# Last product of layer 2: four column blocks over all tokens, four over the left and the right tokens

## The chip, the cores and the metric

The kernel runs on one core of a Trainium2 chip. The metric is the device time of one execution in microseconds: the median of three runs for the kernel before, and one further execution that was profiled. The engines are TensorE (PE, and PEld for its weight loads), VectorE (DVE), ScalarE (ACT), GpSimd (POOL) and SyncE (SP); SP and ACT also issue the DMA transfers of this kernel.

## The reference

Two layers work on 512 tokens of width 1024, then a final RMSNorm. Cut to the part that matters here:

```
h = rmsnorm(x, norm_g)
proj = einsum('bsd,dc->bsc', h, w_in)          # feeds three mixers and three gates
...
pb = einsum('nbsc,ncd->nbsd', ys, w_branch)    # three branch products
gates = sigmoid(gl.reshape(B, S, 3, D))
merged = einsum('bsnd,nbsd->bsd', gates, pb)
x = x + einsum('bsd,de->bse', merged, w_out)   # the last product of a layer
...
out = rmsnorm(x, final_g)                      # after layer 2
```

## The kernel before

All activations lie transposed: features on the 128 partitions, the 512 tokens along the row. A product is done in three matmuls for float32 accuracy: each operand is split into a hi and a lo half, and `mm3` (lines 416 to 419) adds hi x hi, hi x lo and lo x hi into PSUM. The last product of a layer, `i_out` (line 789), makes eight column blocks `e` of 128 output features from eight input chunks `kc`, so 24 matmuls for a block. "Merged" chunks are the inputs: `mg` for chunks 0 to 5, `mgh` and `mgl` (hi and lo) for 6 and 7.

Weights arrive as units of 512 KB (`raw`, two buffers, loaded on SP's queue by `load`, line 138). Each unit has two halves, and `slot` (line 151) splits a half: ScalarE copies it rounded (`whi`, line 159), VectorE or, for one in five, GpSimd subtracts (`wlo`, line 160). There are six `whi` buffers and five `wlo` buffers (lines 154 and 155). `take` hands split halves to a product, `spent` says that one is used, and `ahead` then writes further splits into the program. A load buffer comes free when both halves of its unit are split.

In layer 1 a block covers all 512 tokens, and its halves are spent as it goes. In layer 2 the program goes through the eight blocks twice, first for the left 256 tokens (`LT`), then for the right 256 (`RT`), so that the final norm of the left tokens can be computed beside the right blocks. The weights therefore stay for both passes. Blocks 0 to 2 stay in the `whi` and `wlo` buffers; blocks 3 to 6 go into `xh` and `xl`, the layer's old input activations (no longer read by then), and block 7 into `mh` and `ml`:

```
if g[0] == "O" and g[1] >= NSLOT // 2 and l == DEPTH - 1:
    k = 2 * g[1] + i - NSLOT
    if k < KC:
        dst = xh[:, k, :], xl[:, k, :]
```

For each block the residual `xr` is loaded on ACT's queue (line 795, two buffers), VectorE evicts PSUM into `xf` and adds it (line 810, PSUM tiles `ps_to` in four banks), ScalarE squares it (line 275) and GpSimd adds the squares up (line 279). `final` (line 821) then sums the squares over the features by matmuls with a column of ones (line 394), takes the power on GpSimd (line 401), spreads the result over the partitions (lines 408 and 413), scales the eight blocks on VectorE (line 826) and writes them out, four on SP's queue and four on ACT's (line 827). `final(LT)` stands in the program behind the first right block.

Every engine runs its instructions in the order that a scheduler has set when the program is built. `slot` asks for high priority (`PRIO`), so splits come early in that order. A scheduled instruction waits at the head of its engine's queue until its inputs and buffers are ready, and what stands behind it waits too.

Of the kernel before, what the change touches and what calls it, by code (L numbers as in the profile page):

```python
# [14 lines left out]
ALU = mybir.AluOpType  # L15
# [5 lines left out]
S = 512  # L21
DEPTH = 2
KC = D // P
# [72 lines left out]
NSLOT = 6  # L96
# [3 lines left out]
def hybrid_kernel(ctx: ExitStack, tc, xT, posr, wpack, tabs, cvec, pvec, rvec, lamv, sguw, outT):  # L100
    nc = tc.nc
    V, A, G, T = nc.vector, nc.scalar, nc.gpsimd, nc.tensor
# [16 lines left out]
    def t2k(tag, bufs=2, dt=F32, name=None):  # L119
        return tmp.tile([P, S], dt, tag=tag, bufs=bufs, name=name or tag)  # L120

    def t4k(tag, bufs, dt=F32, name=None):
        return att.tile([P, 2, S], dt, tag=tag, bufs=bufs, name=name or tag)
# [7 lines left out]
    def ps_to():  # L131
        return to_p.tile([P, S], F32, tag="to", name="ps_to")
# [5 lines left out]
    def load():  # L138
        while loaded[0] < min(split_up[0] + RAWB, NU * DEPTH):
            raws[loaded[0]] = raw = wp.tile([P, 1024], F32, tag="raw", bufs=RAWB, name="raw")  # L140
            nc.sync.dma_start(out=raw, in_=wpack[loaded[0]])
            loaded[0] += 1
# [8 lines left out]
    def slot(src, dst=None):  # L151
        if dst is None:
            made[0] += 1
            hi = wp.tile([P, S], F32R, tag="whi", bufs=NSLOT, name="whi")
            lo = wp.tile([P, S], F32R, tag="wlo", bufs=NSLOT - 1, name="wlo")
        else:
            hi, lo = dst
        with tc.high_priority(offset=PRIO):
            A.activation(out=hi, in_=src, func=AF.Copy)  # L159
            (G if made[0] % LOMOD == 0 else V).tensor_tensor(out=lo, in0=src, in1=hi.bitcast(F32), op=ALU.subtract)  # L160
        slots.append((hi, lo))

    def weights():
        for l in range(DEPTH):
            for g in GROUPS:
                u = split_up[0]
                load()
                if g[0] == "S":
                    r1, r2 = raws.pop(u), raws.pop(u + 1)
                    a11, a12, a21, a22 = r1[:, :S], r1[:, S:], r2[:, :S], r2[:, S:]  # L170
                    t12, t34 = t4k("pr", 2, name="t12"), t4k("pr", 2, name="t34")
                    s1, s2, s3, s4 = t12[:, 0, :], t12[:, 1, :], t34[:, 0, :], t34[:, 1, :]
                    slot(a11)
                    yield
                    slot(a12)
                    yield
                    slot(a22)
                    with tc.high_priority(offset=PRIO):
                        SE[0].tensor_tensor(out=s1, in0=a21, in1=a22, op=ALU.add)
                        SE[1].tensor_tensor(out=s2, in0=s1, in1=a11, op=ALU.subtract)  # L180
                        SE[2].tensor_tensor(out=s3, in0=a11, in1=a21, op=ALU.subtract)
                        SE[3].tensor_tensor(out=s4, in0=a12, in1=s2, op=ALU.subtract)
                    split_up[0] += 2
                    load()
                    yield
                    for src in (s2, s3, s1, s4):
                        slot(src)
                        yield
                    continue
                raw = raws.pop(u)  # L190
                for i in range(2):
                    dst = None
                    if g[0] == "O" and g[1] >= NSLOT // 2 and l == DEPTH - 1:
                        k = 2 * g[1] + i - NSLOT
                        if k < KC:
                            dst = xh[:, k, :], xl[:, k, :]
                        else:
                            k = 2 * (k - KC)
                            dst = tuple(t[:, 0, k : k + 2, :].rearrange("p k c -> p (k c)") for t in (mh, ml))
                    slot(raw[:, i * S : i * S + S], dst)  # L200
                    if i == 1:
                        split_up[0] += 1
                        load()
                    yield

    wgen = weights()

    def ahead(n=NSLOT):
# [4 lines left out]
    def take(n):  # L213
        while len(slots) < n:
            next(wgen)
        out = slots[:n]
        del slots[:n]
        return out

    def spent(n):  # L220
        used[0] += n
        ahead()
# [14 lines left out]
    xh = per.tile([P, KC, S], F32R, name="xh")  # L237
    xl = per.tile([P, KC, S], F32R, name="xl")
    mh = per.tile([P, 4, 4, 256], F32R, name="mh")
    ml = per.tile([P, 4, 4, 256], F32R, name="ml")  # L240
# [163 lines left out]
    def rms_spread(rp):  # L404

        n = rp.shape[-1]
        dg = t2k("ob", name="dg")[:, : n * P]
        V.tensor_tensor(
            out=dg.rearrange("p (b j) -> p b j", b=n), in0=ident.unsqueeze(1).to_broadcast([P, n, P]),
            in1=rp.unsqueeze(2).to_broadcast([P, n, P]), op=ALU.mult,  # L410
        )
        bc = ps_s()[:, : n * P]
        T.matmul(bc, lhsT=ones, rhs=dg, start=True, stop=True)
        return bc

    def mm3(ps, wh, wl, mh, ml, first, last):
        T.matmul(ps, lhsT=wh, rhs=mh, start=first, stop=False)  # L417
        T.matmul(ps, lhsT=wh, rhs=ml, start=False, stop=False)  # L418
        T.matmul(ps, lhsT=wl, rhs=mh, start=False, stop=last)  # L419
# [5 lines left out]
    def proj_T(ps, src):  # L425
        for i, (wh, wl) in enumerate(take(2)):
            wh, wl = (w.rearrange("p (k c) -> p k c", k=4) for w in (wh, wl))
            for k in range(4):
                kc = 4 * i + k
                mm3(ps, wh[:, k, :], wl[:, k, :], *src(kc), kc == 0, kc == KC - 1)  # L430
                if k == 3:
                    spent(1)
                yield 0.65
# [61 lines left out]
    LT, RT = slice(0, 256), slice(256, 512)  # L495
# [62 lines left out]
    def layer(l, xu, parts):  # L558
        last = l == DEPTH - 1
# [226 lines left out]
        def merged(kc):  # L786
            return mg[kc // 2][0][:, kc % 2, :], mg[kc // 2][1][:, kc % 2, :]

        def i_out():
            xn[0] = x_ = X()  # L790
            parts = []
            for c in [LT, RT] if last else [slice(0, S)]:
                for e in range(8):
                    xr = t2k("sh", name="xr")[:, c]
                    nc.scalar.dma_start(out=xr, in_=(xT[e, :, c] if l == 0 else x1d[e, :, c]))
                    ps = ps_to()[:, c]
                    if not last:
                        yield from proj_T(ps, merged)
                    else:
                        if c is LT:  # L800
                            parts.append(take(2))
                        for i, (wh, wl) in enumerate(parts[e]):
                            wh, wl = (w.rearrange("p (k c) -> p k c", k=4) for w in (wh, wl))
                            for k in range(4):
                                kc = 4 * i + k
                                mh, ml = merged(kc)
                                mm3(ps, wh[:, k, :], wl[:, k, :], mh[:, c], ml[:, c], kc == 0, kc == KC - 1)
                                yield 0.325
                    xf = (x_.raw(e) if c.start == 0 else x_.f[e // 2][:, e % 2, :])[:, c]
                    V.scalar_tensor_tensor(out=xf, in0=ps, scalar=0.5, in1=xr, op0=ALU.mult, op1=ALU.add)  # L810
                    if last:
                        x_.square(e, c, True)
                    else:
                        x_.take(e, l + 1)
                        nc.sync.dma_start(out=x1d[e], in_=xf)
                    if c is RT and e == 0:
                        final(LT)
            if last:
                final(RT)

        def final(c):
            x_ = xn[0]
            bc = rms_spread(rms_sum([x_.ss[:, c], x_.sq[:, c]]))
            for e in range(KC):
                xf = x_.f[e // 2][:, e % 2, c]
                V.scalar_tensor_tensor(out=xf, in0=xf, scalar=fg[:, e : e + 1], in1=bc, op0=ALU.mult, op1=ALU.mult)
                (nc.sync, nc.scalar)[e % 2].dma_start(out=outT[e, :, c], in_=xf)
# [222 lines left out]
    x1d = dr.tile([KC, P, S], F32, name="x1d")  # L1050
# [88 lines left out]
```

## Time and profile before

| what | us |
|---|---|
| median of three runs (lowest 1148.14, highest 1153.46) | 1151.81 |
| profiled execution | 1150.43 |
| its span on the core | 1148.7 |
| TensorE busy in the span | 1107.1 (96%) |
| VectorE busy | 821.6 (72%) |
| ScalarE busy | 601.7 (52%) |
| GpSimd busy | 515.7 (45%) |

The span holds all instructions of the execution; 1.73 us of the execution lie outside it. The mean granted clock of TensorE over the span is 0.987 of full speed. A busy share is an average over stages, and the product of this change fills only the last part of the span, from about 1076 to 1138 us. A matmul's end in the trace is modelled and overlaps the next one, so the time of a matmul in a stream is read as the distance between two starts.

### The profile page before, as it was taken

Reading aid. Unit: us, or ns where it says so; the run is one execution under the profiler, and the core shown is the slowest. Engines: PE = TensorE matmul, PEld = TensorE weight load, DVE = VectorE, ACT = ScalarE, POOL = GpSimd, SP = SyncE. Lnnn points to the kernel's source line nnn. Section 1 sums busy time; section 2 is a strip of 40 time slices with the busy share of each in tenths; the row PEclk is TensorE's granted clock in tenths of the full one; section 3 lists DMA queues with packets and bytes.
Section 4 is the critical chain, followed back from the end, with each engine's and each line's share of the span. In section 5 each row is a group of like instructions: output and inputs, shape, how many; then the busy total and the mean of one; then the engine's idle time right before and its main releaser. Section 6 shows DMA issues by size and latency. Waiting matters only on the chain.

```text
span 1148.7 us, 18512 instructions
## 1 busy us (share of the span) xinstructions
PE 1107.1 (96%) x6732; PEld 964.8 (84%) x6732; DVE 821.6 (72%) x1503; ACT 601.7 (52%) x1293; POOL 515.7 (45%) x487
## 2 busy tenths in 40 slices
PE   6989999999999999999997999999999999999977
PEld 4768889978779999998886788898787999999976
DVE  5698777567759888874568777746787887877533
ACT  5665655555855444444456464646677544544321
POOL 6664453135333766653342534322343365766312
PEclk9999999999999999999998999999999999999989
DMA  6222211221212332334523121313121133332423
GB/s 199 93 92 79 88 71 59 92 74 56 74 52 96 110 105 80 110 120 139 200 74 91 56 92 56 95 52 96 52 93 56 56 111 110 93 110 80 132 93 101
DMA packets 35643, 106.01 MB, mean 92 GB/s; under 512 B 4768, under 2 KB 8864, under 8 KB 35552
## 3 DMA queue, kind: packets, MB, share of 16 engines
q1 hardware_dynamic: 29936, 98.50, 26.7%
q10 hardware_dynamic: 5616, 6.34, 1.7%
q8 instruction: 53, 0.87, 0.3%
q14 instruction: 38, 0.31, 0.1%
HBM read 100.57 MB, written 4.24 MB: 91 GB/s over the span
## 4 chain that ended last, share of the span: by engine, by line
PE 83%; DVE 6%; POOL 3%; DMA 3%; issue 3%; ACT 2%; POOLq 0%; DVEq 0%; ACTq 0%
PE ps_pj L417 15%; PE ps_pj L419 14%; PE ps_pj L418 14%; PE ps_to L417 8%; PE ps_to L419 8%; PE ps_to L418 8%; PE ps_s L854 4%; PE ps_to L893 2%; PE ps_to L999 2%; PE ps_to L924 1%; DMA raw<-in_wpack 1%; PE ps_pj L441 1%; PE ps_pj L440 1%; PE ps_pj L442 1%; DVE wlo L160 1%
## 5 line engine op out<-in xcount | busy, mean ns | idle before, releaser
L159 ACT ACTIVATE whi<-raw 128x512 fp32r<-128x512 f32 x314 | 194.0, 627 | 240.4 <-DMA raw<-in_wpack 98.5
L160 DVE TENSOR_TENSOR wlo<-raw,whi 128x512 fp32r<-128x512 f32 x251 | 209.4, 839 | 99.8 <-PE ps_pj L419 33.3
L417 PE MATMUL ps_pj<-xh,whi 128*128 128x512 f32 (+1 forms) x544 | 210.9, 388 | 9.2 <-ACT va L707 7.0
L419 PE MATMUL ps_pj<-xh,wlo 128*128 128x512 f32 (+1 forms) x544 | 206.6, 380 | 0.0
L418 PE MATMUL ps_pj<-xl,whi 128*128 128x512 f32 (+1 forms) x544 | 204.9, 377 | 0.0
L160 POOL TENSOR_TENSOR wlo<-raw,whi 128x512 fp32r<-128x512 f32 x63 | 86.9, 1379 | 177.0 <-PE ps_pj L419 69.1
L417 PEld LDWEIGHTS ps_pj<-xh,whi 128*128 128x128 f32 x544 | 103.2, 190 | 30.6 <-ACT va L707 7.8
L419 PEld LDWEIGHTS ps_pj<-xh,wlo 128*128 128x128 f32 x544 | 103.1, 189 | 19.9 <-issue 2.1
L418 PEld LDWEIGHTS ps_pj<-xl,whi 128*128 128x128 f32 x544 | 103.4, 190 | 16.7 <-issue 0.7
L160 DVE TENSOR_TENSOR wlo<-t,whi 128x512 fp32r<-128x512 f32 x90 | 95.5, 1078 | 27.8 <-ACT whi L159 15.7
L159 ACT ACTIVATE whi<-t 128x512 fp32r<-128x512 f32 x112 | 65.6, 624 | 61.1 <-DVE t L180 37.9
L417 PE MATMUL ps_to<-mh,whi 128*128 128x256 f32 x320 | 90.5, 283 | 0.7 <-DVE zs L538 0.7
L418 PE MATMUL ps_to<-ml,whi 128*128 128x256 f32 x320 | 90.5, 283 | 0.0
L419 PE MATMUL ps_to<-mh,wlo 128*128 128x256 f32 x320 | 90.3, 283 | 0.0
L869 ACT ACTIVATE pr<-pr,nm 128x256 f32<-128x256 f32 (+3 forms) x128 | 70.7, 553 | 28.5 <-DVE nm L865 28.2
L471 POOL TENSOR_TENSOR rsh<-rsh,sinr 128x512 f32<-128x512 f32 x32 | 43.7, 1365 | 84.8 <-DVE rsh L469 79.1
L865 DVE CUSTOM_DVE_ANT_0 pr<-ps_s,tab 128x256 f32<-128x256 f32 (+3 forms) x128 | 56.7, 484 | 22.8 <-PE ps_s L854 21.7
L419 PE MATMUL ps_to<-xh,wlo 128*128 128x256 f32 x240 | 67.9, 283 | 0.0
L417 PE MATMUL ps_to<-xh,whi 128*128 128x256 f32 x240 | 67.9, 283 | 0.0
L418 PE MATMUL ps_to<-xl,whi 128*128 128x256 f32 x240 | 67.8, 283 | 0.0
L417 PEld LDWEIGHTS ps_to<-mh,whi 128*128 128x128 f32 x320 | 61.4, 192 | 1.1 <-DVE zs L538 0.9
L774 POOL TENSOR_TENSOR acc<-acc,zs 128x512 f32<-128x512 f32 x32 | 51.6, 1617 | 23.9 <-DVE zs L773 22.7
(260 smaller groups left out, 3022.6 us busy)
## 6 DMA issues: line engine op xcount, KB each, us to landing
raw<-in_wpack SPq DMA_DIRECT2D x174, 512.0 KB
xf<-in_xT SPq DMA_DIRECT2D x8, 256.0 KB
xr<-in_xT ACTq DMA_DIRECT2D x8, 256.0 KB
x1d<-xf SPq DMA_DIRECT2D x8, 256.0 KB
xr<-x1d ACTq DMA_DIRECT2D x16, 128.0 KB
raw<-in_wpack SPq DMA_DIRECT2D x4, 256.0 KB
out<-xf SPq DMA_DIRECT2D x8, 128.0 KB
out<-xf ACTq DMA_DIRECT2D x8, 128.0 KB
```

The costliest lines, as they stand in the source:

```text
L159: A.activation(out=hi, in_=src, func=AF.Copy)
L160: (G if made[0] % LOMOD == 0 else V).tensor_tensor(out=lo, in0=src, in1=hi.bitcast(F32), op=ALU.subtract)
L417: T.matmul(ps, lhsT=wh, rhs=mh, start=first, stop=False)
L418: T.matmul(ps, lhsT=wh, rhs=ml, start=False, stop=False)
L419: T.matmul(ps, lhsT=wl, rhs=mh, start=False, stop=last)
L471: G.tensor_tensor(out=sh, in0=sh, in1=sinr, op=ALU.mult)
L774: G.tensor_tensor(out=acc[d], in0=acc[d], in1=th, op=ALU.add)
L854: T.matmul(pss[m][:, at[i]], lhsT=q[HALF[m], a, qs], rhs=k[HALF[m], b, :W], start=t == 0, stop=t == 2)
L865: V.tensor_tensor_reduce(out=o, in0=pss[m][:, at[i]], in1=tab[:, 0 if br == BR_A else 1, S - W :], op0=ALU.add, op1=ALU.min, scale=-0.125, ...
L869: A.activation(out=o, in_=o, func=AF.Exp, scale=-1.0, bias=nm[:, m : m + 1], accum_out=den[:, m : m + 1],)
L893: T.transpose(pt[:, j, :], pr[:, m, j * P : (j + 1) * P], ident)
L999: T.matmul(po_[m][:, c], lhsT=v[:, j, 2 * h + m, :], rhs=pt[:, j, :], start=j + s_ == 0, stop=j == i and s_ == 1,)
```

## The change

In layer 2 blocks 0 to 3 now run over all 512 tokens, like the blocks of layer 1, and spend their weights as they go. Blocks 4 to 7 run for the left tokens and then for the right tokens. Only their weights are kept, all in `xh` and `xl`. `final(LT)` now stands behind the right part of block 4.

```
-                    if g[0] == "O" and g[1] >= NSLOT // 2 and l == DEPTH - 1:
-                        k = 2 * g[1] + i - NSLOT
-                        if k < KC:
-                            dst = xh[:, k, :], xl[:, k, :]
-                        else:
-                            k = 2 * (k - KC)
-                            dst = tuple(t[:, 0, k : k + 2, :].rearrange("p k c -> p (k c)") for t in (mh, ml))
+                    if g[0] == "O" and g[1] >= KC // 2 and l == DEPTH - 1:
+                        k = 2 * g[1] + i - KC
+                        dst = xh[:, k, :], xl[:, k, :]
...
-            parts = []
-            for c in [LT, RT] if last else [slice(0, S)]:
-                for e in range(8):
-                    xr = t2k("sh", name="xr")[:, c]
-                    nc.scalar.dma_start(out=xr, in_=(xT[e, :, c] if l == 0 else x1d[e, :, c]))
-                    ps = ps_to()[:, c]
-                    if not last:
-                        yield from proj_T(ps, merged)
-                    else:
-                        if c is LT:
-                            parts.append(take(2))
...
-                    if c is RT and e == 0:
-                        final(LT)
+            held = {}
+            todo = [(e, slice(0, S)) for e in range(KC // 2 if last else KC)]
+            if last:
+                todo += [(e, c) for c in (LT, RT) for e in range(KC // 2, KC)]
+            for e, c in todo:
+                xr = t2k("sh", name="xr")[:, c]
+                nc.scalar.dma_start(out=xr, in_=(xT[e, :, c] if l == 0 else x1d[e, :, c]))
+                ps = ps_to()[:, c]
+                if not last or e < KC // 2:
+                    yield from proj_T(ps, merged)
+                else:
+                    if c is LT:
+                        held[e] = take(2)
...
+                if c is RT and e == KC // 2:
+                    final(LT)
```

The order of the instructions is the same in both kernels up to this product. The first place is on VectorE, where the weights of the blocks are split. `raw_11804` is the unit of block 2, and `wlo_11886` the lo part of its second half; `mgl` is the lo part of the last merged chunks, `zs` (line 773, now 769) a gated branch product on its way into them. Before, the last splits are these:

```order
L160 TENSOR_TENSOR xl_93<-raw_12034,xh_92 128x512 x2
L160 TENSOR_TENSOR ml_95<-raw_12072,mh_94 128x512
L810 SCALAR_TENSOR_TENSOR xf_12133<-ps_to_12104,xr_12102 128x256
L160 TENSOR_TENSOR ml_95<-raw_12072,mh_94 128x512
L160 TENSOR_TENSOR wlo_11886<-raw_11804,whi_11885 128x512
L810 SCALAR_TENSOR_TENSOR xf_11985<-ps_to_11960,xr_11958 128x256
```

The split of block 2's second half comes last of all, behind those of blocks 6 and 7. In the changed kernel it stands here:

```order
L769 SCALAR_TENSOR_TENSOR zs_11669<-zs_11669,ps_pj_11849 128x512
L160 TENSOR_TENSOR wlo_11886<-raw_11804,whi_11885 128x512
L769 SCALAR_TENSOR_TENSOR zs_11670<-zs_11670,ps_pj_11872 128x512
L419 TENSOR_TENSOR mgl_11869<-acc_11648,mgh_11868 128x512
L419 TENSOR_TENSOR mgl_11869<-acc_11667,mgh_11868 128x512
L160 TENSOR_TENSOR wlo_11913<-raw_11845,whi_11912 128x512
L160 TENSOR_TENSOR xl_93<-raw_11889,xh_92 128x512 x2
L160 TENSOR_TENSOR wlo_11929<-raw_11845,whi_11928 128x512
```

It has moved ahead of the last merge and of every split of blocks 3 to 7.

The second place is on GpSimd, at the same point of the program: `acc` is the sum over the gated branches (line 774, now 770), and `wlo<-raw` is block 2's other lo split in both kernels. Before:

```order
L160 TENSOR_TENSOR wlo<-raw,whi 128x512
L774 TENSOR_TENSOR acc<-acc,zs 128x512 x3
L160 TENSOR_TENSOR wlo<-raw,whi 128x512
L774 TENSOR_TENSOR acc<-acc,zs 128x512
L279 TENSOR_TENSOR ssum<-ssum,sq 128x256 x8
```

And in the changed kernel:

```order
L160 TENSOR_TENSOR wlo<-raw,whi 128x512
L770 TENSOR_TENSOR acc<-acc,zs 128x512 x2
L160 TENSOR_TENSOR wlo<-raw,whi 128x512
L770 TENSOR_TENSOR acc<-acc,zs 128x512 x2
L275 TENSOR_TENSOR ssum<-ssum,sq 128x512 x3
```

One accumulation has moved from ahead of the split to behind it.

The third place is the end, on VectorE: evictions (line 810, now 808), the norm's `ro` and `dg`, and the scaling (line 826, now 824). Before:

```order
L810 SCALAR_TENSOR_TENSOR xf<-ps_to,xr 128x256 x5
L399 TENSOR_SCALAR ro<-ps_s 128x2
L408 TENSOR_TENSOR dg<-ident,rp 128x256
L810 SCALAR_TENSOR_TENSOR xf<-ps_to,xr 128x256
L826 SCALAR_TENSOR_TENSOR xf<-xf,pv,ps_s 128x256 x8
L810 SCALAR_TENSOR_TENSOR xf<-ps_to,xr 128x256 x4
```

And in the changed kernel:

```order
L808 SCALAR_TENSOR_TENSOR xf<-ps_to,xr 128x512
L808 SCALAR_TENSOR_TENSOR xf<-ps_to,xr 128x256 x5
L395 TENSOR_SCALAR ro<-ps_s 128x2
L404 TENSOR_TENSOR dg<-ident,rp 128x256
L808 SCALAR_TENSOR_TENSOR xf<-ps_to,xr 128x256
L824 SCALAR_TENSOR_TENSOR xf<-xf,pv,ps_s 128x256 x8
L808 SCALAR_TENSOR_TENSOR xf<-ps_to,xr 128x256 x2
```

Two evictions stand behind the eight scalings of the left tokens where four stood.

## Rows read from the trace of the kernel before

**Rows 1.** Stretches: from:to, length, busy per engine (records), clock, DMA share, GB/s.

```profile
539.00:579.00 40.00, 40.00 (x182) 33.22 (x180) 22.54 (x30) 19.44 (x32) 13.25 (x10) 1.00 0.56 185
1083.50:1110.00 26.50, 20.41 (x139) 19.62 (x137) 10.42 (x17) 7.41 (x15) 3.73 (x3) 0.87 0.34 109
1110.00:1138.40 28.40, 28.40 (x236) 28.35 (x236) 9.74 (x23) 5.76 (x14) 8.44 (x12) 1.00 0.25 80
1138.40:1148.70 10.30, 2.18 (x13) 1.41 (x11) 4.23 (x11) 0.42 (x1) 1.09 (x2) 0.73 0.31 102
```

**Rows 2.** Timeline of VectorE, layer 1's evictions: start, length, instruction, [idle before].

```profile
560.24 0.68 DVE L810 SCALAR_TENSOR_TENSOR xf<-ps_to,xr 128x512 f32<-128x512 f32 x1
565.68 0.68 DVE L810 SCALAR_TENSOR_TENSOR xf<-ps_to,xr 128x512 f32<-128x512 f32 x1
```

**Rows 3.** Timeline of TensorE, four pairs: wide, narrow, narrow after a stop, a stop.

```profile
1081.42 0.40 PE L417 MATMUL ps_pj<-y,whi 128*128 128x512 f32 x1
...
1083.24 0.39 PE L419 MATMUL ps_pj<-y,wlo 128*128 128x512 f32 x1
...
1137.31 0.28 PE L419 MATMUL ps_to<-mg,ml 128*128 128x256 f32 x1
...
1138.39 0.28 PE L419 MATMUL ps_to<-mgh,ml 128*128 128x256 f32 x1
...
1095.80 0.41 PE L417 MATMUL ps_to<-mg,xh 128*128 128x256 f32 x1
...
1098.36 0.41 PE L417 MATMUL ps_to<-mg,xh 128*128 128x256 f32 x1
...
1091.26 0.28 PE L419 MATMUL ps_to<-mgh,xl 128*128 128x256 f32 x1
1094.06 0.36 PE L417 MATMUL ps_to<-mg,xh 128*128 128x256 f32 x1 [2.52 <-DVE xf L810]
```

**Rows 4.** Waits from 1083 us on: who, for whom, us, times, longest.

```profile
DVE xf L810 <- DMA xr<-x1d: 13.0, 5, 3.6
ACT xh L159 <- DMA raw<-in_wpack: 12.4, 4, 5.5
...
PE ps_to L417 <- ACT xh L159: 2.8, 1, 2.8
```

**Rows 5.** Timeline of SyncE's loads, ScalarE's splits, and VectorE's late split.

```profile
1087.94 0.33 SPq L141 DMA_DIRECT2D raw<-in_wpack  x1
...
1099.35 0.33 SPq L141 DMA_DIRECT2D raw<-in_wpack  x1
...
1091.62 1.15 ACT L159 ACTIVATE xh<-raw 128x512 fp32r<-128x512 f32 x2 [4.20 <-DMA raw<-in_wpack]
...
1103.69 1.15 ACT L159 ACTIVATE xh<-raw 128x512 fp32r<-128x512 f32 x2 [5.51 <-DMA raw<-in_wpack]
...
1111.97 0.69 DVE L160 TENSOR_TENSOR wlo<-raw,whi 128x512 fp32r<-128x512 f32 x1 [0.36 <-PE ps_to L419]
```

**Rows 6.** Timeline of GpSimd and VectorE at the last merge.

```profile
1083.76 1.30 POOL L160 TENSOR_TENSOR wlo<-raw,whi 128x512 fp32r<-128x512 f32 x1 [0.77 <-ACT mgh L422]
1085.01 1.74 POOL L774 TENSOR_TENSOR acc<-acc,zs 128x512 f32<-128x512 f32 x1
...
1084.34 1.27 DVE L423 TENSOR_TENSOR mgl<-acc,mgh 128x512 fp32r<-128x512 f32 x1
```

**Rows 7.** The chain that ended last, two pieces: start, us, what.

```profile
1101.38 2.61 DMA xr<-x1d
...
1133.55 3.33 DMA xr<-x1d
```

**Rows 8.** The chain's norm sums, then VectorE's scaling and its last eviction.

```profile
1124.17 0.79 PE ps_s L394 x8
...
1129.36 3.22 DVE L826 SCALAR_TENSOR_TENSOR xf<-xf,pv,ps_s 128x256 f32<-128x256 f32 x8 [2.17 <-PE ps_s L413]
...
1138.71 0.42 DVE L810 SCALAR_TENSOR_TENSOR xf<-ps_to,xr 128x256 f32<-128x256 f32 x1 [1.31 <-PE ps_to L419]
```

More of the change, by code (lines that the diff above doesn't have):

```diff
@@ L790, in i_out @@
             xn[0] = x_ = X()
-            parts = []
-            for c in [LT, RT] if last else [slice(0, S)]:
-                for e in range(8):
-                    xr = t2k("sh", name="xr")[:, c]
-                    nc.scalar.dma_start(out=xr, in_=(xT[e, :, c] if l == 0 else x1d[e, :, c]))
-                    ps = ps_to()[:, c]
-                    if not last:
-                        yield from proj_T(ps, merged)
-                    else:
-                        if c is LT:
-                            parts.append(take(2))
[L802 to L815, printed above, removed]
-                    if c is RT and e == 0:
-                        final(LT)
@@ new lines, in i_out @@
+            held = {}
[11 more added lines that the diff above has]
+                        held[e] = take(2)
+                    for i, (wh, wl) in enumerate(held[e]):
+                        wh, wl = (w.rearrange("p (k c) -> p k c", k=4) for w in (wh, wl))
+                        for k in range(4):
+                            kc = 4 * i + k
+                            mh, ml = merged(kc)
+                            mm3(ps, wh[:, k, :], wl[:, k, :], mh[:, c], ml[:, c], kc == 0, kc == KC - 1)
+                            yield 0.325
+                xf = (x_.raw(e) if c.start == 0 else x_.f[e // 2][:, e % 2, :])[:, c]
+                V.scalar_tensor_tensor(out=xf, in0=ps, scalar=0.5, in1=xr, op0=ALU.mult, op1=ALU.add)
+                if last:
+                    x_.square(e, c, True)
+                else:
+                    x_.take(e, l + 1)
+                    nc.sync.dma_start(out=x1d[e], in_=xf)
+                if c is RT and e == KC // 2:
+                    final(LT)
```

## The prediction

> **What bounds the kernel now.** I read the stretches first. TensorE is busy nearly everywhere, so an edit to the last product is worth what TensorE loses there and what follows its last matmul. The same product in layer 1 (512 columns, 539 to 579 us) has TensorE busy 40.00 of 40.00 us, its column blocks evicted every 5.44 us, at a full granted clock [rows 1, 2]. In layer 2 the stretch 1083.5 to 1110 is the poorest before the tail: 20.41 of 26.50 us busy, clock 0.87, 139 matmuls. From 1110 to 1138.4 TensorE is busy throughout; then a tail of 10.3 us has hardly a matmul [rows 1].
>
> Next the matmul spacing, by start times [rows 3]. 512-column matmuls: 1081.42 to 1083.24 is 8 steps, 0.2275 us each. 256-column: 1137.31 to 1138.39 is 9 steps, 0.120 us. The third pair shows them after a stop: 1095.80 to 1098.36 is 12 steps, 0.213 us, the lower of the clock's two levels (1.2 GHz, where 0.120 us goes with 2.4). The fourth pair is such a stop: nothing starts from 1091.26 to 1094.06.
>
> 139 matmuls at 0.120 us are 16.7 us of the 26.5: 9.8 us are lost there, in stops and in matmuls at the lower clock after them. From 1110 on, 236 records stand in 28.4 us. The product has 384 matmuls, 20 of which come before 1083.47 in the order; the surplus over the other 364, some ten records, is the left half's norm sums and spread. 226 x 0.120 = 27.1 us, so these ten cost about 1.3 us and nothing is lost there.
>
> Then who made TensorE stop. Its longest wait is on ScalarE's `xh` split, and ScalarE's `xh` waits 12.4 us in four pieces for weight loads [rows 4]. The loads explain it: SyncE issues one at 1087.94 and the next but one at 1099.35, and the splits start 3.68 and 4.34 us later (1091.62, 1103.69) [rows 5]. There are two load buffers, yet never two loads in flight. The last row of [rows 5] is why: the lo half of block 2's second weight half (`wlo<-raw`) runs only at 1111.97. Five lo slots exist and six would be held, so it waits until the first right block frees one, and holds one load buffer all the while; its row stands behind `ml` in VectorE's order. Blocks 3 to 7 share the other buffer: load, split, load, two turns in 11.4 us, 5.7 each, against 24 x 0.120 = 2.88 us that TensorE needs for a left block.
>
> **The change part by part.** *Widths.* 384 matmuls of 256 columns become 96 of 512 and 192 of 256: 46.1 us become 21.8 + 23.0 = 44.9. Gain 1.2 us. The trace's step exceeds a strict halving by 6 ns per half-width matmul, and that is all of this term. The Trainium skill ("TensorE: Matmul & The Clock Gate", section "Back-to-back issue gap") gives columns/2.4 GHz + 2.5 ns, 215.8 and 109.2 ns, by which the gain would be 0.24 us instead and the whole sum 1.0 us less. The rows here disagree by 12 and 11 ns; the rows decide.
>
> *The held slot.* Blocks 0 to 3 now take their slots and free them as they go, as in layer 1. In the new order of VectorE the same `wlo_11886<-raw_11804` stands ahead of the last merge, and both load buffers rotate. I followed block 4 to 7's weights, at 3.7 us a load and 1.2 us for a ScalarE pair of splits [rows 5]. Block 4's load can start when block 2 is split, near 1086, and lands by 1090; 5 and 6 start near 1094.5 and are in by 1099 to 1101.5 (alone 3.7 us, nearly twice that if two in flight only share); block 7 starts by 1103.5 and is split by 1109. TensorE's needs: the last branch product now ends at 1084.26 (14 wide matmuls come before it instead of 14 + 6 narrow ones: 3.19 - 2.40 = 0.79 later than 1083.47), 82 wide ones follow (18.7 us) up to 1102.9, then a half block every 2.88 us: block 4 at 1102.9, 5 at 1105.8, 6 at 1108.7, 7 at 1111.5. Each is ready at least 2.4 us ahead. Even one load at a time, at 5.7 us a turn from 1086, brings block 7 near 1107. So the four full-width blocks, 21.8 us of matmuls, are the cover, and all of the 9.8 us goes, the low clock too, since nothing stops ahead of it. Bounds: 9.8 us, and nothing. I take 9.8, because layer 1's product streams its weights in this way and loses nothing [rows 1, 2].
>
> *The start.* The product needs the last merged block (`mgh`, `mgl`) after the branch product. POOL's order now has block 2's `wlo` ahead of the last two accumulations instead of between them. It cannot begin before 1084.5 (its slot is the one that the branch product reads): 1.30 us, then two of 1.30 to 1.74 us [rows 6], ends at 1088.4 to 1089.3; ScalarE's copy, half of a 1.15 us pair [rows 5], makes 1089.0 to 1089.9. TensorE has 24 wide matmuls before it asks, 1084.26 + 5.46 = 1089.7. Bounds 0 and 1.0 us (VectorE's `mgl` may last 1.27 us beside POOL [rows 6]); I take 0.2.
>
> *Activations in.* Eight of the sixteen 128 KB loads of `xr` become four of 256 KB. Left unhidden, each would cost its 2.6 to 3.3 us to land [rows 7]; they cost nothing while TensorE has PSUM banks ahead. Blocks 0 and 1's are issued before the product. Blocks 2 and 3's queue on ScalarE behind block 5's splits, so near 1100; they land by 1104, and TensorE wants their banks back (four in all) at 1108.7 and 1111.5.
>
> *The end.* The left half's norm now starts after the first of four right blocks, not of eight, with three left, 8.6 us of matmuls. In the old run, counting from the start of its sums at 1124.17, scaling ended at 1132.58 [rows 8]: 8.4 us. In the new order VectorE has: eviction of right block 5, the eight scalings (3.22 us), evictions of 6 and 7. Right block 4 ends near 1117.6; sums, spread and scaling then run to about 1126.2; block 6's eviction follows, and TensorE finishes block 7 near 1127 (1102.9 + 23.0 + 1.3 = 1127.2). So the last eviction waits little. ScalarE has four output issues ahead of its last two squares; the fourth waits for the eighth scaling. Bounds 0 and 3.6 us (all eight scalings and one eviction in the way); I take 0.2. Behind the last eviction the same instructions follow as now, 1138.71 to 1148.7, so 10.0 us stay.
>
> **Sum.** 1.2 + 9.8 - 0.2 - 0.2 = 10.6 us. The profiled execution took 1150.43 us (span 1148.7 and 1.73 around it), 1.4 under the median of the three runs: 1139.8 against it, 1141.2 against the median. I take 1140.3.
>
> **Rivals.** *The end crowds.* The scalings, or an `xr` behind the outputs, push the last eviction by the full 3.6 us: 1143.9. For it: the chain of the old run passes through a 3.33 us `xr` in just this place, behind the left half's scaling [rows 7, 8]. Against: all four right `xr` issues now stand ahead of the output issues on ScalarE, where two stood behind them. Chance 0.10.
>
> *Weights still come late.* Two loads and the `xr` in flight get in each other's way, block 7 is late and TensorE stops once. One stop cost 2.68 us (1091.26 to 1094.06, less a step) [rows 3] and then, at 0.093 us extra for each of some 16 matmuls, 1.5: 1140.3 + 4.2 = 1144.5. For it: the load with `xr` transfers beside it took 4.34 us, the one without 3.68 [rows 5, 7]. Against: the 2.4 us of slack. The Trainium skill ("DMA: Bandwidth & Descriptors", section "Issuing engines are not separate DMA queues") says that transfers from different engines run on the same 16 engines and interleave; the 4.34 us agrees with that. Chance 0.08.
>
> *It does not do what it says.* The stops return in full in the four left blocks, for a reason in the order that I missed, and only the widths pay: 1140.3 + 9.8 = 1150.1. For it: the left blocks still read weights split just ahead. Against: 21.8 us of cover. Chance 0.05.
>
> *Slower.* The `xr` turn sets the pace of all eight half blocks: eviction, square, issue on ScalarE's queue, landing, eviction, in two buffers. With 0.42 us for an eviction [rows 8], as much for a square by my estimate, and 2.6 to 3.3 us [rows 7] this is at most 4.2 for two blocks, and TensorE takes 5.76 for two. For it: evictions waited 13.0 us for `xr` in five waits [rows 4]. If the turn grew to T, each block would lose (T - 5.76)/2; above 8.4 us the gain is gone, and at 10 us, 17 us are lost: 1157. Nothing in the trace reaches 5.8. Chance 0.03.
>
> **How the numbers follow.** Forecast 0.74, at 1140.3. Less than 0.5% of the median (5.8 us, about what runs of this kernel can tell from no change) means 1146.0 to 1157.6. Faster: 0.74 + 0.10 + 0.08 = 0.92; same 0.05; slower 0.03. The range: 10.6 + 0.4 off the lowest run, 1148.14, gives 1137.1; above, the second rival's single stop, 1144.5. I keep 1137 to 1144.5, which leaves out what lies beyond: the last two rivals and the poorer half of the second, 0.12.
>
> **What would show it.** TensorE without a gap over 0.5 us between 1084 and the last product matmul, granted clock 1.00 in every stretch, that matmul at 1127 to 1128 (1138.39 now); weight loads of blocks 5 and 6 issued within 1 us of each other; `wlo` of block 2 before 1087; half blocks evicted every 2.9 us; 10 us from the last eviction to the end. A gap before block 5, 6 or 7 with ScalarE waiting for a load proves the second rival; a last eviction over 1 us behind its matmul the first; an eviction that waits for `xr` while TensorE waits for its bank the fourth.

## The result, and the profile after

| | before | after |
|---|---|---|
| median of four runs, us | 1151.38 | 1140.12 |
| lowest to highest | 1148.14 to 1153.46 | 1139.28 to 1141.74 |
| profiled execution, its span | 1150.43, 1148.7 | 1140.47, 1138.7 |
| mean granted clock | 0.987 | 0.990 |

The ratio is 0.9899 (95% interval 0.9886 to 0.9912). The forecast was 1140.3 us, with a range of 1137 to 1144.5.

The stretches of the changed kernel, in the columns of [rows 1]:

```profile
539.00:579.00 40.00, 40.00 (x178) 33.12 (x177) 21.88 (x29) 18.37 (x31) 12.06 (x9) 1.00 0.57 185
1083.50:1110.00 26.50, 26.50 (x143) 22.95 (x142) 12.29 (x21) 9.54 (x17) 8.23 (x7) 1.00 0.35 120
1110.00:1128.40 18.40, 18.40 (x154) 18.22 (x152) 6.20 (x16) 2.34 (x6) 3.62 (x5) 1.00 0.27 83
1128.40:1138.70 10.30, 1.83 (x11) 1.26 (x10) 4.23 (x11) 0.57 (x2) 1.43 (x2) 0.73 0.36 121
```

The second line is the change: TensorE busy 26.50 of 26.50 us at clock 1.00, where [rows 1] had 20.41 and 0.87. Layer 1's stretch and the tail are as before. The record counts mean little here, since the new stretch mixes wide and narrow matmuls.

TensorE's timeline at three places: the last full-width stretch, the end of the product, and the norm's first sums behind it.

```profile
1099.90 0.39 PE L413 MATMUL ps_to<-mg,whi 128*128 128x512 f32 x1
...
1103.75 0.39 PE L415 MATMUL ps_to<-mgh,wlo 128*128 128x512 f32 x1
1103.98 0.28 PE L413 MATMUL ps_to<-mg,xh 128*128 128x256 f32 x1
...
1127.84 0.28 PE L415 MATMUL ps_to<-mgh,xl 128*128 128x256 f32 x1
...
1128.20 0.28 PE L415 MATMUL ps_to<-mgh,xl 128*128 128x256 f32 x1
1129.48 0.38 PE L390 MATMUL ps_s<-ones,ssum 128*128 128x1 f32 x2 [1.01 <-POOL ssum L275]
```

From 1099.90 to 1103.75 are 17 steps of 0.2265 us, from 1127.84 to 1128.20 three of 0.120, as in [rows 3]. The last product matmul starts at 1128.20 (1138.39 before). No step in between is more than 0.2 us too long.

Waits from 1083 us on, answering [rows 4]:

```profile
ACT xh L159 <- DMA raw<-in_wpack: 5.9, 3, 4.5
...
DVE wlo L160 <- PE ps_to L415: 2.7, 1, 2.7
...
PE ps_s L390 <- POOL ssum L275: 1.0, 1, 1.0
```

TensorE's wait for `xh` is gone, and so are VectorE's 13.0 us for `xr`. ScalarE still waits for loads, but for 5.9 us instead of 12.4, and TensorE does not wait for ScalarE.

The answer to [rows 5]. SyncE's loads of blocks 4 to 7:

```profile
1086.51 0.33 SPq L141 DMA_DIRECT2D raw<-in_wpack  x1
1092.02 0.33 SPq L141 DMA_DIRECT2D raw<-in_wpack  x1
1095.38 0.33 SPq L141 DMA_DIRECT2D raw<-in_wpack  x1
1097.78 0.33 SPq L141 DMA_DIRECT2D raw<-in_wpack  x1
```

ScalarE's splits of blocks 5 to 7, which wait for them:

```profile
1095.57 0.63 ACT L159 ACTIVATE xh<-raw 128x512 fp32r<-128x512 f32 x1 [4.54 <-DMA raw<-in_wpack]
...
1098.92 1.15 ACT L159 ACTIVATE xh<-raw 128x512 fp32r<-128x512 f32 x2 [1.16 <-DMA raw<-in_wpack]
...
1101.79 1.15 ACT L159 ACTIVATE xh<-raw 128x512 fp32r<-128x512 f32 x2 [0.24 <-DMA raw<-in_wpack]
```

And VectorE's two lo splits that wait for a slot:

```profile
1085.76 0.69 DVE L160 TENSOR_TENSOR wlo<-raw,whi 128x512 fp32r<-128x512 f32 x1 [2.20 <-PE ps_pj L415]
...
1094.66 0.69 DVE L160 TENSOR_TENSOR wlo<-raw,whi 128x512 fp32r<-128x512 f32 x1 [2.66 <-PE ps_to L415]
```

Block 2's second half is split at 1085.76 (1111.97 before). The same thing now happens, much shorter, to block 3: its last lo split waits until 1094.66 for TensorE to free a slot. Until then it keeps one load buffer, so block 5's load follows block 4's in the other one and block 6's follows only at 1095.38. All weights have landed by 1101.8, when ScalarE starts the last splits; TensorE starts the first left block at 1103.98.

**The account.** Up to the product the order of instructions is the same in both kernels, but the starts of a stage differ between executions by a few us. So I measure from a fixed matmul: the last one that reads the old activations as its input (`ps_to<-xh,wlo`, at 1070.00 before and 1071.19 after), on to the last product matmul, and from there to the end of the span.

| kernel | marker | last product matmul | product, us | tail, us |
|---|---|---|---|---|
| before | 1070.00 | 1138.39 | 68.39 | 10.31 |
| after | 1071.19 | 1128.20 | 57.01 | 10.50 |
| before, slot free | 1069.80 | 1129.55 | 59.75 | 10.95 |
| before, six lo buffers | 1077.42 | 1136.12 | 58.70 | 10.38 |
| after, buffer held | 1070.18 | 1133.37 | 63.19 | 13.73 |
| after, narrow | 1071.43 | 1130.04 | 58.61 | 11.06 |
| after, five wide | 1069.89 | 1126.57 | 56.68 | 12.93 |
| after, six wide | 1072.90 | 1128.84 | 55.94 | 12.36 |
| after, left norm late | 1071.49 | 1128.08 | 56.59 | 12.62 |
| after, six lo buffers | 1074.88 | 1131.89 | 57.01 | 11.11 |

The product became 11.38 us shorter and the tail 0.19 longer. The profiled execution of after reached the marker 1.19 later, which makes the 10.0 us between the spans. Each row is one profiled execution.

### The profile page after: what moved, and what is told of

Read it like the earlier page. It is cut to its first block, busy times and chain, and to the rows that moved or that the text cites. A ratio compares the mean times of both kernels' runs of the same rounds, so it can differ in the third digit from the quotient of the medians.

```text
span 1138.7 us, 18298 instructions
## 1 busy us (share of the span) xinstructions
PE 1101.4 (97%) x6636; PEld 955.8 (84%) x6636; DVE 821.1 (72%) x1499; ACT 599.8 (53%) x1289; POOL 513.9 (45%) x484
## 4 chain that ended last, share of the span: by engine, by line
PE 81%; DVE 6%; POOL 4%; issue 3%; DMA 3%; ACT 2%; POOLq 0%; DVEq 0%; ACTq 0%; SPq 0%
PE ps_pj L413 14%; PE ps_pj L415 14%; PE ps_pj L414 14%; PE ps_to L413 8%; PE ps_to L415 8%; PE ps_to L414 8%; PE ps_s L852 4%; PE ps_to L891 2%; PE ps_to L997 2%; DVE wlo L160 2%; DMA raw<-in_wpack 2%; PE ps_to L922 2%; PE ps_pj L437 1%; PE ps_pj L436 1%; PE ps_pj L438 1%
## 5 line engine op out<-in xcount | busy, mean ns | idle before, releaser
L160 DVE TENSOR_TENSOR wlo<-raw,whi 128x512 fp32r<-128x512 f32 x253 | 212.5, 845 | 105.0 <-ACT whi L159 41.0
L415 PEld LDWEIGHTS ps_to<-mh,wlo 128*128 128x128 f32 x320 | 61.3, 192 | 0.7 <-POOL wlo L160 0.4
```

## The experiments

Ratios are to the kernel before, run on the same chip.

**The held buffer alone, taken out of the kernel before.** Two passes over eight blocks as before; only block 2's weights go to the free second half of `mh` and `ml`, so that no lo slot is wanted for them.

```
-                    if g[0] == "O" and g[1] >= NSLOT // 2 and l == DEPTH - 1:
+                    if g[0] == "O" and g[1] >= 2 and l == DEPTH - 1:
                         k = 2 * g[1] + i - NSLOT
-                        if k < KC:
+                        if k < 0:
+                            dst = tuple(t[:, 1, 2 * i : 2 * i + 2, :].rearrange("p k c -> p (k c)") for t in (mh, ml))
+                        elif k < KC:
```

> The kernel before, all sixteen half-width blocks kept, with one edit: block 2's weights also go into mh and ml, so only two blocks stay in the five lo slots and no load buffer is held. Theory H (the held load buffer made TensorE stop): weight loads come in two at a time, a block every 2.8 us or so, which is about what TensorE needs (2.88), so the stretch loses at most 2 us of the 9.8: 1142 to 1144. Rival C (the four full-width blocks are the cover, and without them loads are late however many buffers there are): at least half of the loss stays, 1146 to 1151. Rival W (the widths alone): 1151.

Measured: 1143.53 us, ratio 0.9934 (0.9916 to 0.9951), inside the 1142 to 1144 of theory H. The product takes 59.75 us, 8.64 less than before, with no other edit. Its stretch:

```profile
1083.50:1110.00 26.50, 25.33 (x212) 25.13 (x211) 13.29 (x23) 10.07 (x21) 6.32 (x8) 1.00 0.35 106
```

The loads of blocks 4 to 7, on SyncE:

```profile
1080.72 0.33 SPq L141 DMA_DIRECT2D raw<-in_wpack  x1
1084.99 0.33 SPq L141 DMA_DIRECT2D raw<-in_wpack  x1
1088.50 0.33 SPq L141 DMA_DIRECT2D raw<-in_wpack  x1
1090.51 0.33 SPq L141 DMA_DIRECT2D raw<-in_wpack  x1
```

And the one stop that is left on TensorE (1092.26 to 1093.70), with what ScalarE and VectorE do meanwhile:

```profile
1091.96 1.15 ACT L159 ACTIVATE xh<-raw 128x512 fp32r<-128x512 f32 x2 [2.29 <-DMA raw<-in_wpack]
...
1092.26 0.28 PE L421 MATMUL ps_to<-mgh,xl 128*128 128x256 f32 x1
...
1092.62 0.69 DVE L160 TENSOR_TENSOR xl<-raw,xh 128x512 fp32r<-128x512 f32 x1 [2.15 <-ACT xh L159]
1093.23 0.75 DVE L812 SCALAR_TENSOR_TENSOR xf<-ps_to,xr 128x256 f32<-128x256 f32 x2
...
1093.70 0.39 PE L419 MATMUL ps_to<-mg,xh 128*128 128x256 f32 x1 [1.17 <-DVE xf L812]
```

Loads come 2 to 4.3 us apart instead of two in 11.4, and the clock is 1.00. So the held buffer made nearly all the stops, and the full-width blocks are not needed to remove them. The stop that is left cost 1.43 us: its step is 1.44, or 1.32 over 0.120, and the next step is 0.11 too long. TensorE there waits for an eviction: the eviction stands on VectorE behind an `xl` split, and that split waits for ScalarE and the load. This is the second way in which a late load reaches TensorE: through PSUM banks that stay full. [Rows 3]'s stop ended on VectorE's `xf` too.

**The held buffer put back into the changed kernel.** A further `raw` tile takes one of the two load buffers ahead of block 4's load, the one that comes free first, and lets it go behind the last left block; a write and a read of one column each are all that it does.

```
+            if loaded[0] == NU * DEPTH - 4:
+                hold.append(wp.tile([P, 1024], F32, tag="raw", bufs=RAWB, name="hold"))
+                V.memset(hold[0][:, 0:1], 0.0)
...
+                if c is LT and e == KC - 1:
+                    V.tensor_tensor(out=sm.tile([P, 1], F32, tag="free", name="free"), in0=hold[0][:, 0:1], in1=xf[:, 0:1], op=ALU.add)
```

> The changed kernel with one load buffer held from block 4's load to the last left block (a one-column write and read of a third tile): blocks 4 to 7 load one at a time, as before the change. The prediction's claim that even one load at a time hides behind the four wide blocks: 1140. Theory H: block 4's load can start only when block 3 is split (1095.4 in the changed kernel's trace), then 5 us a turn; blocks 6 and 7 come 1.5 and 3 us late, with a stretch at the lower clock: 1143 to 1146. If cover counts for nothing: the whole 9.8 back, 1150.

Measured: 1149.29 us, ratio 0.9982 (0.9971 to 0.9993). The product is 6.18 us longer than in the changed kernel, the tail 3.23. The time is near the 1150 of the last case expected, but not for its reason: the product gives back 6.18 us, more than theory H had and less than the whole, and the rest is the tail. The stretch in which the left blocks run:

```profile
1110.00:1128.00 18.00, 15.21 (x110) 14.81 (x111) 4.59 (x10) 4.17 (x9) 2.55 (x4) 0.91 0.20 61
```

The loads of blocks 4 to 7, on SyncE:

```profile
1094.44 0.33 SPq L145 DMA_DIRECT2D raw<-in_wpack  x1
1100.69 0.33 SPq L145 DMA_DIRECT2D raw<-in_wpack  x1
1106.92 0.33 SPq L145 DMA_DIRECT2D raw<-in_wpack  x1
1112.32 0.33 SPq L145 DMA_DIRECT2D raw<-in_wpack  x1
```

One of the two stops on TensorE:

```profile
1115.87 0.28 PE L419 MATMUL ps_to<-mgh,xl 128*128 128x256 f32 x1
1117.69 0.39 PE L417 MATMUL ps_to<-mg,xh 128*128 128x256 f32 x1 [1.54 <-ACT xh L163]
```

And VectorE at the end:

```profile
1132.74 3.22 DVE L830 SCALAR_TENSOR_TENSOR xf<-xf,pv,ps_s 128x256 f32<-128x256 f32 x8 [1.93 <-PE ps_s L413]
1135.88 0.42 DVE L812 SCALAR_TENSOR_TENSOR xf<-ps_to,xr 128x256 f32<-128x256 f32 x1
```

With one load buffer, in a chain that starts at 1094.44, the four full-width blocks do not cover the loads. Block 4's load cannot go out before block 3 is split, at 1094.44, 8 us later than in the changed kernel, and the turns are 5.4 to 6.2 us. The tail shows something else: here the left tokens' scalings ended up ahead of the last eviction, which starts 2.5 us behind the last product matmul (1133.37).

**Widths alone, taken out of the changed kernel.** Blocks 0 to 3 keep their weights' order and their PSUM bank, but run 256 columns twice (one pass for the left, one for the right half).

```
+                if last and e < KC // 2:
+                    pair2 = take(2)
+                    for h in (LT, RT):
+                        ...
+                        mm3(ps[:, h], wh[:, k, :], wl[:, k, :], mh[:, h], ml[:, h], kc == 0, kc == KC - 1)
```

> The changed kernel with blocks 0 to 3 done as a left and a right half-width pass over the same weights, one after the other, into one PSUM bank: 384 matmuls of 256 columns again, the loads, stores and norms as in the changed kernel. The trace's steps (0.2275 and 0.120 us): 96 pairs cost 1.2 us more, 1141.3. The page's formula: 0.24 us more, 1140.4. If half-width passes themselves brought the stops: 1145 or more.

Measured: 1143.01 us, ratio 0.9930 (0.9915 to 0.9945). That is above the 1141.3 expected from the steps. The product is 1.60 us longer than with wide matmuls, and the tail 0.56. In the timeline 0.29 of the product is TensorE waiting for `mgl` early on, which the narrow form asks for sooner; 1.31 is left for the widths, 13.6 ns for each of the 96 pairs. The edit is not quite the widths alone: GpSimd's last lo split stands between the accumulations again, as before the change, and block 4's load goes out only at 1092.45. No stop follows, nor does the single stop of the first experiment come.

**Six blocks at full width, two left and right.**

```
+WIDE = 6
...
-            todo = [(e, slice(0, S)) for e in range(KC // 2 if last else KC)]
+            todo = [(e, slice(0, S)) for e in range(WIDE if last else KC)]
...
-                    todo += [(e, c) for c in (LT, RT) for e in range(KC // 2, KC)]
+                    todo += [(e, c) for c in (LT, RT) for e in range(WIDE, KC)]
```

> The changed kernel with blocks 0 to 5 over all tokens and only 6 and 7 over left and right. Theory E (the left norm needs cover by right blocks): one right block, 2.9 us, stands behind the left norm's 8.4 us, so about 5.5 us are laid bare, less 0.6 from two more wide blocks: 1144 to 1146. Rival (the end is not bound by the norm's cover): 1139.5.

Measured: 1141.54 us, ratio 0.9915 (0.9895 to 0.9934). The product is 1.07 us shorter, the tail 1.86 longer. Of the 1.07, 0.42 is the left norm's spread, which now stands behind the last product matmul; 0.65 is left for the 48 pairs, 13.5 ns each. Both theories missed: the cover of the left norm is worth something, but less than feared. VectorE at the end, the last eviction, the left scalings, and the right norm's first step:

```profile
1129.16 0.42 DVE L813 SCALAR_TENSOR_TENSOR xf<-ps_to,xr 128x256 f32<-128x256 f32 x1 [0.89 <-PE ps_to L420]
1129.60 3.22 DVE L829 SCALAR_TENSOR_TENSOR xf<-xf,pv,ps_s 128x256 f32<-128x256 f32 x8
1132.74 0.15 DVE L400 TENSOR_SCALAR ro<-ps_s 128x2 f32<-128x2 f32 x1
```

The last eviction is in time; the eight scalings then stand ahead of the right norm's `ro`, which has no idle time in front of it.

**Five blocks at full width.** The same edit with `WIDE = 5`.

> The changed kernel with five column blocks at full width and three over the left and the right tokens. Widths: 24 wide matmuls in place of 48 narrow ones, 0.4 us by the measured 1.6 us for four blocks, 0.5 by the six-wide run's 1.07 for two. Against it the end: with two right blocks behind the left norm in place of three, 5.8 us of matmuls instead of 8.6 to cover 8.4 us of sums, spread and scaling. If the cover is priced evenly between the run with four (tail 10.5 us) and the run with six (12.4), the tail grows by 0.9 and the kernel comes out at 1140.5; if the last block alone hides most of it, tail +0.2 and 1139.8. Either way within 0.5% of the changed kernel.

Measured: 1142.23 us, ratio 0.9920 (0.9906 to 0.9935). The product is 0.33 us shorter, near the 0.4 to 0.5 expected (24 pairs, 13.8 ns each), but the tail grows by 2.43, not by 0.2 to 0.9:

```profile
1125.78 3.22 DVE L829 SCALAR_TENSOR_TENSOR xf<-xf,pv,ps_s 128x256 f32<-128x256 f32 x8 [1.77 <-PE ps_s L414]
1128.92 0.42 DVE L813 SCALAR_TENSOR_TENSOR xf<-ps_to,xr 128x256 f32<-128x256 f32 x1
```

Here the scalings come ahead of the last eviction, whose matmul started at 1126.57. The price does not grow evenly with the number of blocks; in these rows it goes by where the order puts the eight scalings. Four wide blocks have the lowest time of the three forms, but the intervals overlap, so no order among the three is shown.

**The left norm behind the third right block.** Nothing else is changed.

```
-                if c is RT and e == KC // 2:
+                if c is RT and e == KC - 2:
                     final(LT)
```

> The changed kernel with the left tokens' norm put behind the third right block instead of the first: one right block, 2.9 us of matmuls, is left to cover it, as in the six-wide run. This measures the price of the cover alone. By the six-wide run the tail grows by 1.9 us: 1142.0. If the full 3.6 us of the prediction's first rival stand before the last eviction: 1143.7. If TensorE's and VectorE's order hides it all the same: 1140.2. The last product itself stays at 57.0 us in each case.

Measured: 1142.37 us, ratio 0.9917 (0.9903 to 0.9932), near the 1142.0 that the six-wide run had led to expect. The product takes 56.59 us, the tail 12.62, which is 2.12 more:

```profile
1128.40 0.42 DVE L808 SCALAR_TENSOR_TENSOR xf<-ps_to,xr 128x256 f32<-128x256 f32 x1 [0.88 <-PE ps_to L415]
1128.83 3.22 DVE L824 SCALAR_TENSOR_TENSOR xf<-xf,pv,ps_s 128x256 f32<-128x256 f32 x8
1131.97 0.15 DVE L395 TENSOR_SCALAR ro<-ps_s 128x2 f32<-128x2 f32 x1
```

The picture is that of six wide blocks. So the tail's growth there came from the missing cover, not from the widths. The product is 0.42 shorter because the left norm's spread now stands behind its last matmul.

**Six lo buffers in the kernel before.**

```
-            lo = wp.tile([P, S], F32R, tag="wlo", bufs=NSLOT - 1, name="wlo")
+            lo = wp.tile([P, S], F32R, tag="wlo", bufs=NSLOT, name="wlo")
```

> The kernel before with six lo buffers (wlo) in place of five; nothing else. Theory (the held buffer: five lo slots, six wanted by blocks 0 to 2, so that block 2's second half keeps a load buffer until 1112): the second half of block 2 is split as soon as its weights are there, loads come in pairs, and most of the 8.6 us that the first experiment won come back: the last product takes 59 to 61 us where 68.4 were, about 1142 to 1144. The order of earlier stages shifts too with a sixth buffer, which may move the time by 1 or 2 us either way. Rival (the second pass as such, or late loads for another reason, makes TensorE stop): 1149 to 1151, with loads still 11 us apart for two.

Measured: 1146.35 us, ratio 0.9953 (0.9935 to 0.9971), above the 1142 to 1144 expected. In the product the theory holds: 58.70 us, 9.69 less than before, a little better than the 59 to 61 expected, and the stretch that answers to 1083.5 to 1110 (6.5 us later here) is full:

```profile
1090.00:1116.50 26.50, 26.38 (x219) 26.10 (x218) 13.90 (x23) 9.77 (x20) 7.12 (x9) 1.00 0.39 121
```

The longest stop of TensorE in this product is the following step of 0.41 us, 0.29 too long; the step behind it costs another 0.09:

```profile
1096.52 0.28 PE L418 MATMUL ps_to<-mg,xh 128*128 128x256 f32 x1
1096.93 0.62 PE L417 MATMUL ps_to<-mgh,whi 128*128 128x256 f32 x3
```

All sixteen half-width blocks are still there, and yet the 1.43 us stop of the first experiment is absent. So that stop belongs to the first experiment's order of loads and splits; it is not the price of half-width blocks.

But the marker comes 7.4 us later than before. 1.4 of that is there at layer 1's last eviction (572.49 against 571.12), the rest grows in layer 2 ahead of the product.

**Six lo buffers in the changed kernel.** The same line.

> The changed kernel with six lo buffers in place of five. In its last product TensorE stops nowhere, so the theory expects nothing from there: 1138.5 to 1140.5, no difference that can be told. Load of block 5 is to move towards that of block 6, since block 3's second half need not wait for a lo slot (both within 1.5 us, where 3.4 us were). Rival (the lo slots hold TensorE up in earlier stages too): 1136 or less.

Measured: 1143.25 us, ratio 0.9922 (0.9907 to 0.9938), so slower than forecast. The product takes 57.01 us, the same as without, and the loads of blocks 5 and 6 go out together:

```profile
1095.43 0.33 SPq L141 DMA_DIRECT2D raw<-in_wpack  x1
1096.03 0.33 SPq L141 DMA_DIRECT2D raw<-in_wpack  x1
```

That gains nothing, since TensorE waited for neither. From layer 1's last eviction to the marker it takes 503.5 us (504.9 in the run before this one), where before and after take 498.9 and 498.2, and the six other kernels 498.1 to 499.1. The sixth buffer costs about 5 us of these profiled executions in layer 2's earlier stages, whose order it changes; the median lies only 3.1 us above that of the changed kernel. Which instruction there pays was not settled.

## Why the prediction was right, and where it was not

**The account adds up.** Before to after, the product lost 11.38 us. Three kernels do it in half-width matmuls with hardly a stop, by different edits. Less the waits that are left in each, they agree: the first experiment 59.75 - 1.43, six lo buffers in the kernel before 58.70 - 0.38, the third experiment 58.61 - 0.29, each 58.32 us. So stops and low clock in the kernel before were 68.39 - 58.32 = 10.07 against 9.8 forecast, and the widths 58.32 - 57.01 = 1.31 against 1.2. With nothing paid at the start and 0.19 at the end the account gives 11.19 and the medians differ by 11.26, against 10.6 forecast. That the time still came within 0.2 us of 1140.3 is in part luck: the 10.6 were taken off 1150.9, which is below the median of 1151.38.

**Widths.** Right. The formula of the Trainium skill ("TensorE: Matmul & The Clock Gate", section "Back-to-back issue gap"), which the section gives for a single isolated matmul, would have given 0.24 us. The third experiment measures 1.31, and the wide step of 0.2265 us stands 11 ns above its figure. The rows were the better guide.

**Held slot.** The cause was right: two experiments on the kernel before take the held buffer away by different edits, and each frees 8.6 to 9.7 us of the product. The reason that the prediction gave for the new order was wrong in two places. First, "the four full-width blocks, 21.8 us of matmuls, are the cover, and all of the 9.8 us goes": the first experiment has no such cover and gets most of it back, and six lo buffers, also without it, get back all but 0.38 us. Two load buffers that turn are enough here; the cover is not needed. Second, "even one load at a time, at 5.7 us a turn from 1086, brings block 7 near 1107": with one buffer, block 7's load went out at 1112.32 and 6.18 us were lost. That sentence took 1086 as the start of the chain. It left out that block 3's second half needs a lo slot, which TensorE frees only in the course of the first wide blocks, so that the buffer not held starts its next load at 1094.44. A chain of single loads that does start near 1086 was not run. The forecast of blocks 5 and 6 within 1 us of each other failed the other way: block 6 went out at 1095.38, near the 1094.5 forecast, but block 5 already at 1092.02, behind block 4 in the buffer that was turning. Nothing was late, and no stop came in the left blocks, so the second and third rivals are out.

**Start.** 0.2 forecast, nothing paid:

```profile
1089.49 0.69 DVE L419 TENSOR_TENSOR mgl<-acc,mgh 128x512 fp32r<-128x512 f32 x1 [1.85 <-ACT mgh L418]
...
1091.74 0.39 PE L414 MATMUL ps_to<-mgl,whi 128*128 128x512 f32 x1
```

`mgl` is done at 1090.18, and TensorE first reads it at 1091.74, so the margin was over 1.5 us. It begins the chunks with `mgh` at 1090.83, without a gap. The third experiment, which asks earlier, pays 0.29. One premise was wrong: GpSimd's lo split began at 1082.97, not after 1084.5. But the last accumulation then waited 1.68 us for VectorE's `zs`, which stands behind block 2's second lo split.

**Activations in.** Right: no wait for `xr` is left after 1083, and the left half blocks are evicted every 2.88 us. The fourth rival is out. Most of that wait went with the held buffer: the first experiment keeps all sixteen small loads, and there it falls from 13.0 to 2.8 us.

**The end.** Right in size, +0.19 against 0.2, by another path. VectorE in the changed kernel, answering to [rows 8]:

```profile
1122.34 0.42 DVE L808 SCALAR_TENSOR_TENSOR xf<-ps_to,xr 128x256 f32<-128x256 f32 x1 [0.88 <-PE ps_to L415]
1124.45 3.22 DVE L824 SCALAR_TENSOR_TENSOR xf<-xf,pv,ps_s 128x256 f32<-128x256 f32 x8 [1.69 <-PE ps_s L409]
1127.59 0.41 DVE L808 SCALAR_TENSOR_TENSOR xf<-ps_to,xr 128x256 f32<-128x256 f32 x1
1128.51 0.42 DVE L808 SCALAR_TENSOR_TENSOR xf<-ps_to,xr 128x256 f32<-128x256 f32 x1 [0.51 <-PE ps_to L415]
```

The scalings delay the eviction of right block 6 to 1127.59, as forecast: near 1126.2, plus the 1.19 by which the marker is later. The last eviction (1128.51) is on time with 0.51 us to spare. The 0.2 comes from GpSimd, which adds up the delayed block's squares, and for which TensorE waits 1.01 us (the right norm's `ro` starts 2.37 us behind the last product matmul, 2.17 before). The first rival's price, 3.6 us, was near what came once in full in the held-buffer run (3.23); three runs with less cover paid 1.9 to 2.4.

## What to carry over

Count the buffers that a pass holds against those that the pool has: a producer that cannot get its output buffer keeps its input buffer too, and what you then see in the waits is a slow load. When a chain of loads is forecast, start it from the event that frees the buffer it runs in, not from the first load of any buffer. Work placed to be hidden should be judged by its place in the order of the engine that the tail needs: 0.5 us of slack held in one form, and one block less cost 2.4.

## What was not expected of the hardware

A sixth buffer made the kernel slower ahead of the product by about 5 us in the profiled executions, though in the kernel before it removes a wait in the product. This looks like the scheduler's doing rather than the chip's, since VectorE's order differs from the first 100 us on. And a load that is late reaches TensorE by two ways here: by the split it waits for (the 1.54 us wait in the held-buffer run), and by evictions that stand behind that split on VectorE (the 1.17 us wait in the first experiment, the 2.52 us wait before the change). A stop does not always bring the low clock: the first experiment's stop of 1.32 us left the granted clock of its stretch at 1.00, while in the kernel before, with stops of 2.68 and 2.99 us, it was 0.87.
